# At the border between attention and MLP: other places for the norm's sum, the residual's scaling, the sums of z's quarters and the reciprocal

## The chip, the cores and the metric

The kernel runs on one core of a Trainium2 chip. The core has a matrix engine (TensorE, PE in the profile; its weight loads are listed apart as PEld), a vector engine (VectorE, DVE), an activation engine (ScalarE, ACT), a general engine (GpSimd, POOL) and an engine that here only issues transfers (SyncE, SP). Each works through its own list of instructions in order and waits on semaphores where an instruction needs another engine's result or a transfer. The metric is the device time of one execution in microseconds; the kernel before has a median of 644.58 us over three runs (643.77 to 645.73).

## The reference, cut to what matters

One decoder layer for 512 tokens of width 1024, all in float32: attention in three groups of heads, then a squared-ReLU MLP, each behind an RMS norm and each added to the residual.

```
def rms_norm(x, gain):
    y = xf * lax.rsqrt(jnp.mean(xf * xf, axis=-1, keepdims=True) + EPS)
    return (y * gain)

def mixer_sublayer(...):
    ...
    y = jnp.concatenate([y_moba, y_fox, y_dil], axis=-1) @ w_out
    return x + y

def mlp_sublayer(x, norm_g, w_up, w_down):
    hn = rms_norm(x, norm_g)
    return x + jnp.square(jax.nn.relu(hn @ w_up)) @ w_down
```

w_up is 1024 x 4096 and w_down 4096 x 1024. Since the MLP's activation is the square of a ReLU, the norm's factor 1/sqrt(v) (v is a token's mean square plus epsilon) can be left out of the products and comes out as 1/v at the end.

## The kernel before, in words

**Products in three passes.** Every float32 operand is split into a high and a low part of a type that TensorE multiplies in one pass, and a product is hi*hi + hi*lo + lo*hi. ScalarE writes a weight tile's high part (`whi`, L118), VectorE its low part (`wlo`, L119: raw minus high). Both lie in three buffers; a `Stream` object splits two pieces ahead of TensorE and loads further ahead, and a buffer is written again when TensorE has finished with the tile three before.

**Up to the border.** After attention, `x2` is the residual (eight tiles of 128 features x 512 tokens). `out_product` adds W_out's result to it in four parts; as the last two parts finish, `out_done` makes of each tile: zf (x2 times the norm's gain), its parts zh and zl, and its square. The squares of four tiles each are to be added up in two tiles `ssq`: ScalarE writes the first square into it, and the other three (`sq`, four buffers) are added by a GpSimd transfer with an adding destination (L757), so three and three transfers, each waiting for the one before it on the same tile.

**The MLP.** Its first block of 512 hidden features is an ordinary product (`up0`): 32 steps of three matmuls, four accumulators; steps 0 to 7 use weights k = 0, 1, steps 8 to 23 k = 2 to 5, steps 24 to 31 k = 6, 7, where an accumulator is finished at steps 25, 27, 29 and 31 and goes through `up_done` (copy to `c`, L853; square, L841; high part, L844; low part, L845). Then follow eight periods u = 1 to 8. In a period the up products of block u are done by a scheme of seven half-size products in place of eight (numbers 1 to 7, 24 matmuls each, L872) between four down items of block u - 1 (d00, d01, d10, d11; 24 matmuls each, L913), in the order `PERIOD = (1, 5, "d00", 2, 6, "d01", 3, 7, "d10", 4, "d11")`. The seven products need sums of z's quarters: `t_sum` (L806, VectorE) builds them for products 5, 6, 7 and 4, `t_split` (L818 ScalarE, L819 VectorE) their parts t5, t6, t7 and, for 4, a new zh and zl.

**The norm.** `x2_stats` multiplies the two `ssq` tiles with a tile of ones (L825, two float32 products in a bank of PSUM) and makes v2 (L826). `scale_x2` multiplies each tile of x2 by v2 (L831); the down results are added to that (L922), and near the end everything is multiplied by rv = 1/v2 (`RECIPROCAL`, L943).

**What sets the order.** TensorE's instructions stand in the order in which the program writes them. The instructions of the other engines are put in order by a scheduler, which keeps an instruction's needs ahead of it but can move it to and fro; `keep_in_program_order` holds one at the place where it is written. Tiles of a pool that is closed are given to pools opened later: pool `zfp` (zf, ssq, sq) is closed after step 20 of `up0`, and pool `hp` (h tiles, `c`) takes its place, so that the first write to a `c` waits for the transfers that read `sq`.

Of the kernel before, what the change touches and what calls it, by code (L numbers as in the profile page):

```python
# [11 lines left out]
F32 = mybir.dt.float32  # L12
# [6 lines left out]
P = 128  # L19
D = 1024  # L20
S = 512
# [135 lines left out]
def hymba_block(ctx: ExitStack, tc: tile.TileContext, a, out):  # L157
    nc = tc.nc
# [9 lines left out]
    def bank(tag):  # L168
        return psum.tile([P, 512], F32, name=tag, tag=tag)
# [23 lines left out]
    for c in range(len(IN_CHUNKS)):  # L193
        src = a[f"w_in{c}"]
        n = src.shape[2]
# [39 lines left out]
    for u in range(1, 9):  # L235
        for what in PERIOD:
            if isinstance(what, str):
                c, p = int(what[1]), int(what[2])
                k = 4 * (u - 1) + 2 * p
# [7 lines left out]
    def product(first, ks, operands, banks_n, done, G=2):  # L247


        n = len(ks)  # L250
        acc = [None] * banks_n
        head, tail = list(range(min(G, n))), list(range(max(G, n - G), n))
        mid = [k for k in range(n) if k not in head and k not in tail]
        order = [(k, b) for b in range(banks_n) for k in head]
        order += [(k, b) for k in mid for b in range(banks_n)]
        order += [(k, b) for b in range(banks_n) for k in tail]
        if first == 0:

            wh, wl = w.take(0)
            acc = [bank("acc") for _ in range(banks_n)]  # L260
            for m in (0, 2, 1):
                for b in range(banks_n):
                    pairs, view = operands(ks[0], b, wh, wl)
                    lhs, rhs = pairs[m]
                    nc.tensor.matmul(view(acc[b]), lhsT=lhs, rhs=rhs, start=(m == 0), stop=False)
            order = [(k, b) for k, b in order if k > 0]
        for k, b in order:
            wh, wl = w.take(first + k)
            if acc[b] is None:
                acc[b] = bank("acc")  # L270
            pairs, view = operands(ks[k], b, wh, wl)
            dst = view(acc[b])
            for m, (lhs, rhs) in enumerate(pairs):
                nc.tensor.matmul(  # L274
                    dst, lhsT=lhs, rhs=rhs, start=(k == 0 and m == 0), stop=(k == n - 1 and m == 2)
                )
            if k == n - 1:
                done(b, acc[b])
            yield
# [428 lines left out]
    for c, (kind, i) in enumerate(IN_CHUNKS):  # L708
        done = {"g": lambda i: g_done, "qk": lambda i: qk_parts[i][0], "v": v_done}[kind](i)
        n = a[f"w_in{c}"].shape[2]  # L710
# [65 lines left out]
    v2 = mlp.tile([P, S], F32, name="v2")  # L776
    rv = mlp.tile([P, S], F32, name="rv")
# [2 lines left out]
    zstack = ExitStack()  # L780
    zpool = zstack.enter_context(tc.tile_pool(name="zfp", bufs=1, side="right"))
    zf = zpool.tile([P, NK, S], F32, name="zf")
    ssq = [zpool.tile([P, S], F32, name=f"ssq{m}") for m in range(2)]
    for c, part, ks in OUT_ORDER[2:]:
        for _ in product(out_first[c, part], ks, out_operands, 4, out_done(c, part)):
            pass
# [11 lines left out]
    def t_sum(n):  # L798
        t = mlp_pools["sum"].tile([P, 4, HALF], F32, name="wsum")
        first, second = {  # L800
            5: (zf[:, lo4, t1], zf[:, lo4, t0]),
            6: (zf[:, hi4, t1], tsum.get(5)),
            4: (zf[:, hi4, t0], tsum.get(6)),
            7: (zf[:, hi4, t1], zf[:, lo4, t1]),
        }[n]
        nc.vector.tensor_tensor(t, first, second, op=ALU.subtract)  # L806
        tsum[n] = t
        if n == 4:

            hi, lo = zh[:, lo4, t1], zl[:, lo4, t1]  # L810
        else:
            hi, lo = (tp.tile([P, 4, HALF], F32R, name=f"t{n}{m}") for m in "hl")
        zop[n] = (hi, lo)
        return n

    def t_split(n):
        hi, lo = zop[n]
        nc.scalar.copy(hi, tsum[n])  # L818
        nc.vector.tensor_tensor(lo, tsum[n], hi.bitcast(F32), op=ALU.subtract)  # L819

    def x2_stats():

        ps = bank("m")
        for m in range(2):
            nc.tensor.matmul(ps, lhsT=ones, rhs=ssq[m], start=(m == 0), stop=(m == 1))  # L825
        nc.vector.tensor_scalar(v2, ps, 1.0 / D, EPS, op0=ALU.mult, op1=ALU.add)  # L826

    def scale_x2(k):


        nc.vector.tensor_tensor(x2[:, k], x2[:, k], v2, op=ALU.mult)  # L831
# [3 lines left out]
    def h_tiles(u):  # L835
        for p in range(2):
            h_at[u, p] = [hp.tile([P, 2, S], F32R, name=f"h{m}{p}", bufs=2) for m in "hl"]
# [21 lines left out]
    def up_product(u, n):  # L859

        wh, wl = w.take_made(up_first[u, n])
        bh, bl = zop[n]
        slot, first = {1: ("x", True), 6: ("x", False), 7: ("x", False), 4: ("x", False),
                       5: ("v", True), 3: ("v", False), 2: ("y", True)}[n]
        if first:
            slots[slot] = bank("m")
        acc = slots[slot]
        for f in range(2):
            for j in range(4):
                lh, ll = (x[:, j, f * P : (f + 1) * P] for x in (wh, wl))  # L870
                for m, (lhs, rhs) in enumerate(((lh, bh[:, j]), (lh, bl[:, j]), (ll, bh[:, j]))):
                    nc.tensor.matmul(  # L872
                        acc[:, f * HALF : (f + 1) * HALF], lhsT=lhs, rhs=rhs,
                        start=first and (f, j, m) == (0, 0, 0), stop=(f, j, m) == (1, 3, 2), skip_group_check=True,
                    )
        up_parts(u, n, acc)
# [24 lines left out]
    def down_item(q, c, p):  # L901
        hi, lo = h_at[q, p]
        first = down_first[q, c, p]
        if p == 0:
            down_acc[c] = [None] * 4
        for b in range(4):
            if p == 0:
                down_acc[c][b] = bank("acc")
            acc = down_acc[c][b]
            for k in range(2):  # L910
                wh, wl = (x[:, b * P : (b + 1) * P] for x in w.take(first + k))
                for m, (lhs, rhs) in enumerate(((wh, hi[:, k]), (wh, lo[:, k]), (wl, hi[:, k]))):
                    nc.tensor.matmul(acc, lhsT=lhs, rhs=rhs, start=(p, k, m) == (0, 0, 0), stop=(p, k, m) == (1, 1, 2))  # L913
            if p == 1:
                down_done(q, c, b, acc)
# [10 lines left out]
                (nc.sync, nc.scalar)[m].dma_start(rows[:, cols], dst[:, cols])  # L926

    for n, _ in enumerate(product(up0_first, list(range(NK)), up_operands, 4, up_done)):
        if n == 0:
            for m in (5, 6, 7):  # L930
                t_sum(m), t_split(m)
            t_sum(4)
        if n == 20:
            x2_stats()
            zstack.close()
            hp = ctx.enter_context(tc.tile_pool(name="hp", bufs=1, side="right"))
            h_tiles(0)
    t_split(4)
    for u in range(1, 9):
        if u < 8:  # L940
            h_tiles(u)
        if u == 5:
            nc.vector.reciprocal(rv, v2)  # L943
        for what in PERIOD:
            if isinstance(what, str):
                down_item(u - 1, int(what[1]), int(what[2]))
            elif u < 8:
                up_product(u, what)
            if u == 1 and what in (1, 5):
                for k in range(4):  # L950
                    scale_x2(k + (4 if what == 5 else 0))


def bias_tables():
# [64 lines left out]
```

## Time and profile before

| | us |
|---|---|
| median of three runs | 644.58 |
| the three runs | 644.58, 643.77, 645.73 |
| the profiled execution | 646.33 |
| its span, first to last instruction | 644.6 |
| TensorE busy in the span | 631.2 (98%) |
| VectorE busy | 460.6 (71%) |
| ScalarE busy | 322.5 (50%) |
| GpSimd busy | 43.7 (7%) |
| mean granted clock of TensorE, of full speed | 0.995 |

The trace was taken in one execution; its times count from the span's start. Busy shares are means over stages of different kinds. A line of the timeline gives an instruction's start, its duration, its engine, line, operation and tiles, and in brackets how long the engine was idle before it and what ended that. TensorE's matmuls overlap, so their pace is read from the distance of starts, not from durations. The chain of waits lists what released what, from the span's end backwards.

### The profile page before, as it was taken

Reading aid. Unit: us, or ns where it says so; the run is one execution under the profiler, and the core shown is the slowest. Engines: PE = TensorE matmul, PEld = TensorE weight load, DVE = VectorE, ACT = ScalarE, POOL = GpSimd, SP = SyncE. Lnnn points to the kernel's source line nnn. Section 1 sums busy time; section 2 is a strip of 40 time slices with the busy share of each in tenths; the row PEclk is TensorE's granted clock in tenths of the full one; section 3 lists DMA queues with packets and bytes.
Section 4 is the critical chain, followed back from the end, with each engine's and each line's share of the span. In section 5 each row is a group of like instructions: output and inputs, shape, how many; then the busy total and the mean of one; then the engine's idle time right before and its main releaser. Section 6 shows DMA issues by size and latency. Waiting matters only on the chain.

```text
span 644.6 us, 9830 instructions
## 1 busy us (share of the span) xinstructions
PE 631.2 (98%) x3800; PEld 558.4 (87%) x3800; DVE 460.6 (71%) x786; ACT 322.5 (50%) x575; POOL 43.7 (7%) x63
## 2 busy tenths in 40 slices
PE   7999999999999999999799999999999999999997
PEld 6798898898898998887599889898989899989886
DVE  6794695696588564769799766677586766865872
ACT  7457765766776676359244333333334333434320
POOL 4010210120120100001000000000000000000000
PEclk8999999999999999999899999999999999999999
DMA  8524333433421453276316143232522333212213
GB/s 315 160 91 138 115 83 75 123 91 112 118 83 50 118 160 116 67 262 130 99 33 196 40 158 99 75 99 89 164 84 60 120 99 130 66 34 67 67 39 125
DMA packets 24911, 70.03 MB, mean 109 GB/s; under 512 B 3210, under 2 KB 4762, under 8 KB 24864
## 3 DMA queue, kind: packets, MB, share of 16 engines
q1 hardware_dynamic: 18224, 57.84, 28.2%
q10 hardware_dynamic: 4432, 5.77, 3.7%
q0 software_dynamic: 2208, 5.79, 3.7%
q8 instruction: 30, 0.49, 0.3%
q14 instruction: 17, 0.14, 0.1%
HBM read 61.51 MB, written 2.11 MB: 99 GB/s over the span
## 4 chain that ended last, share of the span: by engine, by line
PE 72%; DVE 7%; ACT 3%; DMA 3%; issue 1%; POOL 0%; ACTq 0%; DVEq 0%; POOLq 0%
PE acc L913 28%; PE m L872 22%; PE acc L274 16%; DMA ssq<-sq 3%; PE m L514 2%; PE m L565 2%; PE m L541 1%; DVE ptl L548 1%; PE m L495 1%; DVE qkss L400 1%; DVE wlo L119 1%; DVE qks L418 1%; DVE m L526 1%; DVE qkraw L413 1%; ACT whi L118 1%
## 5 line engine op out<-in xcount | busy, mean ns | idle before, releaser
L118 ACT CAST whi<-wraw 128x1024 fp32r<-128x1024 f32 (+3 forms) x66 | 66.6, 1013 | 87.1 <-PE acc L913 40.5
L274 PE MATMUL acc<-whi,xh 128*128 128x512 f32 (+3 forms) x284 | 103.5, 364 | 0.7 <-DVE fl L436 0.4
L913 PE MATMUL acc<-hh,wlo 128*128 128x512 f32 x256 | 101.4, 396 | 0.0
L913 PE MATMUL acc<-hl,whi 128*128 128x512 f32 x256 | 101.3, 396 | 0.0
L913 PE MATMUL acc<-hh,whi 128*128 128x512 f32 x256 | 101.0, 395 | 0.0
L119 DVE TENSOR_TENSOR wlo<-wraw,whi 128x1024 fp32r<-128x1024 f32 (+3 forms) x66 | 78.9, 1197 | 30.2 <-ACT whi L118 29.5
L274 PE MATMUL acc<-wlo,xh 128*128 128x512 f32 (+3 forms) x284 | 95.7, 337 | 0.7 <-DVE wlo L119 0.6
L274 PE MATMUL acc<-whi,xl 128*128 128x512 f32 (+3 forms) x284 | 95.8, 337 | 0.0
L872 PE MATMUL m<-zh,whi 128*128 128x256 f32 x224 | 62.5, 279 | 0.0
L872 PE MATMUL m<-zh,wlo 128*128 128x256 f32 x224 | 62.4, 278 | 0.0
L872 PE MATMUL m<-zl,whi 128*128 128x256 f32 x224 | 62.4, 278 | 0.0
L274 PEld LDWEIGHTS acc<-whi,xl 128*128 128x128 f32 x284 | 53.6, 189 | 5.2
L913 PEld LDWEIGHTS acc<-hh,wlo 128*128 128x128 f32 x256 | 48.3, 189 | 10.8
L274 PEld LDWEIGHTS acc<-wlo,xh 128*128 128x128 f32 x284 | 54.0, 190 | 3.7 <-DVE wlo L119 1.5
L913 PEld LDWEIGHTS acc<-hl,whi 128*128 128x128 f32 x256 | 48.3, 189 | 10.1
L274 PEld LDWEIGHTS acc<-whi,xh 128*128 128x128 f32 x284 | 53.7, 189 | 3.8 <-DVE vs L430 0.7
L913 PEld LDWEIGHTS acc<-hh,whi 128*128 128x128 f32 x256 | 48.3, 189 | 9.9
L118 ACT CAST whi<-wsum 128x1024 fp32r<-128x1024 f32 x28 | 29.4, 1049 | 49.9 <-PE m L872 36.4
L119 DVE TENSOR_TENSOR wlo<-wsum,whi 128x1024 fp32r<-128x1024 f32 x28 | 34.1, 1220 | 23.0 <-ACT whi L118 23.0
L922 DVE TENSOR_TENSOR x<-acc,x 128x512 f32<-128x512 f32 (+1 forms) x65 | 42.5, 677 | 10.3 <-PE acc L913 9.6
L528 ACT ACTIVATE p<-m,mn 128x128 f32<-128x128 f32 (+1 forms) x64 | 33.6, 527 | 24.4 <-DVE mn L526 22.7
L872 PEld LDWEIGHTS m<-zh,whi 128*128 128x128 f32 x224 | 42.1, 188 | 1.2
(189 smaller groups left out, 1330.0 us busy)
## 6 DMA issues: line engine op xcount, KB each, us to landing
wraw<-in_w_down SPq DMA_DIRECT2D x32, 512.0 KB, 3.6
ublk<-in_w_up SPq DMA_DIRECT2D x28, 512.0 KB, 4.0
wraw<-in_w_in SPq DMA_DIRECT2D x21, 512.0 KB, 3.9
stk<-stk ACTq DMA_DIRECT2D x32, 128.0 KB, 2.3
wraw<-in_w_out SPq DMA_DIRECT2D x6, 512.0 KB, 4.1
alibi<-in_alibi POOLq DMA_DIRECT2D x10, 256.0 KB, 3.4
x<-in_xT SPq DMA_DIRECT2D x4, 512.0 KB, 5.8
wraw<-in_w_up SPq DMA_DIRECT2D x4, 512.0 KB, 4.9
```

What stands on the lines that cost most here:

```text
L118: nc.scalar.copy(hi, raw)
L119: nc.vector.tensor_tensor(lo, raw, hi.bitcast(F32), op=ALU.subtract)
L274: nc.tensor.matmul(dst, lhsT=lhs, rhs=rhs, start=(k == 0 and m == 0), stop=(k == n - 1 and m == 2))
L400: nc.vector.tensor_reduce(ss, sq.rearrange("p (h d) -> p h d", d=DH), axis=AX.X, op=ALU.add)
L413: nc.vector.tensor_tensor(raw, raw, state["y"][:, t].unsqueeze(2).broadcast_to([P, 8, DH]), op=ALU.mult)
L418: nc.vector.tensor_tensor(split[:, :, 1], raw, split[:, :, 0].bitcast(F32), op=ALU.subtract)
L514: nc.tensor.matmul(ps[:, :n], lhsT=st[0][:, i * P : (i + 1) * P], rhs=st[m][:, :n], start=(m == 1), stop=(m == 2 and h < FOX0),)
L528: nc.scalar.activation(p, ps[:, :n], AF.Exp, bias=mn, scale=-1.0, accum_out=st["den"][:, i : i + 1])
L565: nc.tensor.matmul(ot[:, j * P :], lhsT=v, rhs=p, start=(half == 0 and j == 0), stop=(half == 1 and j == 3))
L872: nc.tensor.matmul(acc[:, f * HALF : (f + 1) * HALF], lhsT=lhs, rhs=rhs, start=first and (f, j, m) == (0, 0, 0), stop=(f, j, m) == (1, 3, ...
L913: nc.tensor.matmul(acc, lhsT=lhs, rhs=rhs, start=(p, k, m) == (0, 0, 0), stop=(p, k, m) == (1, 1, 2))
L922: nc.vector.tensor_tensor(dst[:, cols], acc[:, cols], dst[:, cols], op=ALU.add)
```

## The change

Five edits. The two `ssq` tiles no longer have memory of their own but use v2's and rv's. The sums and splits of z's quarters for products 5, 6 and 7 are written at steps 8, 13 and 18 of `up0` instead of all at step 0, and that for product 4 at step 20. The two products with ones move from behind step 20 of `up0` to behind product 5 of period 1. The eight scalings of x2 are written behind products 2 and 6 of period 1 instead of behind 1 and 5. The reciprocal is held at the place where it is written, the start of period 5.

```diff
-    ssq = [zpool.tile([P, S], F32, name=f"ssq{m}") for m in range(2)]
+    ssq = [v2, rv]
...
     for n, _ in enumerate(product(up0_first, list(range(NK)), up_operands, 4, up_done)):
-        if n == 0:
-            for m in (5, 6, 7):
-                t_sum(m), t_split(m)
-            t_sum(4)
+        if n in (8, 13, 18):
+            m = {8: 5, 13: 6, 18: 7}[n]
+            t_sum(m), t_split(m)
         if n == 20:
-            x2_stats()
+            t_sum(4)
             zstack.close()
...
         if u == 5:
-            nc.vector.reciprocal(rv, v2)
+            tc.keep_in_program_order(nc.vector.reciprocal(rv, v2))
...
-            if u == 1 and what in (1, 5):
+            if u == 1 and what == 5:
+                x2_stats()
+            if u == 1 and what in (2, 6):
                 for k in range(4):
-                    scale_x2(k + (4 if what == 5 else 0))
+                    scale_x2(k + (4 if what == 6 else 0))
```

Three places show what the scheduler makes of it. First VectorE in the middle of `up0`: `t5l` to `t7l` belong to the quarters' sums, `wlo<-wraw` are the low parts of `up0`'s weights for k = 4, 5 and for k = 6, 7, `wlo<-ublk` those of period 1's product 1.

```order
 L749 TENSOR_TENSOR zl<-zf,zh 128x512
+L119 TENSOR_TENSOR wlo<-wraw,whi 128x1024
 L819 TENSOR_TENSOR t5l<-wsum,t5h 128x1024
 L819 TENSOR_TENSOR t6l<-wsum,t6h 128x1024
+L119 TENSOR_TENSOR wlo<-wraw,whi 128x1024
 L806 TENSOR_TENSOR wsum<-zf 128x1024
-L119 TENSOR_TENSOR wlo<-wraw,whi 128x1024 x2
+L119 TENSOR_TENSOR wlo<-ublk,whi 128x1024
 L819 TENSOR_TENSOR t7l<-wsum,t7h 128x1024
```

The first low part of a weight moves up past three instructions (t5l, t6l and the sum for product 7), the second past one. On ScalarE the high part for k = 4, 5 moves up past the high parts of t5 and t6 in the same way.

Second ScalarE at the end of `up0`, before and then now: `zh<-wsum` is product 4's high part, `whi<-wsum` the weights' high part of period 1's product 5, `c<-acc` the copies of `up0`'s results.

```order
L818 CAST zh_3456<-wsum_3662 128x4x256
L118 CAST whi_3775<-wsum_3773 128x1024
L853 COPY c_3782<-acc_3640 128x512
L853 COPY c_3793<-acc_3671 128x512
L844 CAST hh0_3751<-c_3782 128x512
```

```order
L818 CAST zh_3456<-wsum_3739 128x4x256
L853 COPY c_3776<-acc_3638 128x512
L118 CAST whi_3769<-wsum_3767 128x1024
L853 COPY c_3787<-acc_3649 128x512
L844 CAST hh0_3745<-c_3776 128x512
```

The first copy, which waits for the adding transfers, now stands ahead of product 5's weights.

Third VectorE from the last result of `up0` into period 1, before and then now: `wlo_3827` and `wlo_3821` are d00's weights, `wlo_3933` and `wlo_3923` d01's, `x2<-x2,v2` the scalings.

```order
L831 TENSOR_TENSOR x2_3016<-x2_3016,v2_3458 128x512 x3
L119 TENSOR_TENSOR wlo_3894<-ublk_3726,whi_3893 128x1024
L216 TENSOR_TENSOR wsum_3902<-wsum_3773,ublk_3638 128x1024
L943 RECIPROCAL rv_3459<-v2_3458 128x512
L119 TENSOR_TENSOR wlo_3905<-wsum_3902,whi_3904 128x1024
L119 TENSOR_TENSOR wlo_3933<-wraw_3768,whi_3932 128x1024
```

```order
L119 TENSOR_TENSOR wlo_3821<-wraw_3674,whi_3820 128x1024
L845 TENSOR_TENSOR hl1_3748<-c_3809,hh1_3747 128x512
L119 TENSOR_TENSOR wlo_3884<-ublk_3716,whi_3883 128x1024
L218 TENSOR_TENSOR wsum_3992<-ublk_3716,wsum_3892 128x1024
L826 TENSOR_SCALAR v2_3458<-m_3878 128x512
L119 TENSOR_TENSOR wlo_3895<-wsum_3892,whi_3894 128x1024
L831 TENSOR_TENSOR x2_3016<-x2_3016,v2_3458 128x512 x8
L119 TENSOR_TENSOR wlo_3923<-wraw_3762,whi_3922 128x1024
```

The eight scalings, before spread from the middle of `up0` on, now stand in one row directly ahead of d01's weights, and the reciprocal has left this place; it stands in period 5, directly ahead of that period's d00 weights. From period 2 on the engines' lists are otherwise as they were.

## Rows read from the trace of the kernel before

**Rows 1.** Chain of waits around the border: start us, us, engine, tiles, line.

```profile
293.81 5.99 DMA ssq<-sq
300.87 4.30 DMA ssq<-sq
305.70 4.04 DMA ssq<-sq
310.27 3.29 DMA ssq<-sq
313.60 1.13 PE m L825 x2
```

**Rows 2.** Waits of TensorE: who waited for whom, us in total, times, longest.

```profile
PE m L825 <- DMA ssq<-sq: 2.8, 1, 2.8
...
PE acc L274 <- DVE wlo L119: 1.9, 2, 1.2
```

**Rows 3.** Timeline of TensorE through `up0`: start us, us, what [idle before].

```profile
294.50 0.39 PE L274 MATMUL acc<-zh,whi 128*128 128x512 f32 x1
...
305.04 0.39 PE L274 MATMUL acc<-zl,whi 128*128 128x512 f32 x1
306.63 0.51 PE L274 MATMUL acc<-zh,wlo 128*128 128x512 f32 x1 [1.20 <-DVE wlo L119]
...
309.74 1.02 PE L825 MATMUL m<-ssq,ones 128*128 128x512 f32 x2
313.60 1.13 PE L825 MATMUL m<-ssq,ones 128*128 128x512 f32 x2 [2.85 <-DMA ssq<-sq]
...
323.72 0.28 PE L872 MATMUL m<-zh,whi 128*128 128x256 f32 x1
```

**Rows 4.** Stretches: us, busy of each engine, then TensorE's granted clock, DMA, GB/s.

```profile
306.00:309.00 3.00, 2.37 (x10) 1.98 (x11) 3.00 (x4) 0.78 (x1) 0.56 (x1) 1.00 0.68 82
...
314.00:318.00 4.00, 4.00 (x11) 2.87 (x10) 2.42 (x3) 0.00 (x0) 0.00 (x0) 0.59 0.00 0
```

**Rows 5.** The same view, periods 1 and 2.

```profile
323.70:366.10 42.40, 42.40 (x267) 38.19 (x266) 39.00 (x47) 17.44 (x23) 0.00 (x0) 1.00 0.33 100
366.10:408.30 42.20, 42.20 (x267) 38.01 (x266) 29.75 (x35) 16.01 (x20) 0.00 (x0) 1.00 0.32 100
```

**Rows 6.** Timeline of VectorE, the same columns as rows 3.

```profile
301.00 0.69 DVE L749 TENSOR_TENSOR zl<-zf,zh 128x512 fp32r<-128x512 f32 x1 [0.70 <-ACT zh L748]
...
304.23 1.22 DVE L806 TENSOR_TENSOR wsum<-zf 128x1024 f32<-128x1024 f32 x1
305.36 2.35 DVE L119 TENSOR_TENSOR wlo<-wraw,whi 128x1024 fp32r<-128x1024 f32 x2
...
329.12 1.90 DVE L831 TENSOR_TENSOR x<-x,v 128x512 f32<-128x512 f32 x3
...
333.20 3.35 DVE L943 RECIPROCAL rv<-v 128x512 f32<-128x512 f32 x1
...
494.04 1.22 DVE L119 TENSOR_TENSOR wlo<-wraw,whi 128x1024 fp32r<-128x1024 f32 x1
```

**Rows 7.** Timeline of ScalarE.

```profile
300.87 1.04 ACT L818 CAST t5h<-wsum 128x1024 fp32r<-128x1024 f32 x1
...
302.77 2.00 ACT L118 CAST whi<-wraw 128x1024 fp32r<-128x1024 f32 x2
...
319.80 0.59 ACT L853 COPY c<-acc 128x512 f32<-128x512 f32 x1 [0.66 <-PE acc L274]
```

**Rows 8.** Timeline of SyncE's queue: loads that the low parts released.

```profile
306.61 0.33 SPq L95 DMA_DIRECT2D wraw<-in_w_down  x1
307.74 0.33 SPq L95 DMA_DIRECT2D wraw<-in_w_down  x1
```

**Rows 9.** Timeline of TensorE at d00 of period 5.

```profile
498.52 0.40 PE L913 MATMUL acc<-hh,wlo 128*128 128x512 f32 x1
```

More of the change, by code (lines that the diff above doesn't have):

```diff
@@ L928, in hymba_block @@
     for n, _ in enumerate(product(up0_first, list(range(NK)), up_operands, 4, up_done)):
-        if n == 0:
-            for m in (5, 6, 7):
-                t_sum(m), t_split(m)
+        if n in (8, 13, 18):
+            m = {8: 5, 13: 6, 18: 7}[n]
+            t_sum(m), t_split(m)
+        if n == 20:
             t_sum(4)
-        if n == 20:
-            x2_stats()
             zstack.close()
```

## The prediction

> **What bounds the kernel now.** I read the chain of waits first. It ends in TensorE from the border on: from 313.60 us nothing but matmuls stands in it, and ahead of that four adding transfers ssq<-sq and the second product with ones [rows 1]. So every microsecond that TensorE stands still or runs slowly at the border is a microsecond of the whole, and nothing else there is. The stretches of the MLP say the same: in periods 1 and 2 TensorE is busy for the full 42.40 and 42.20 us, with VectorE at 39.00 and 29.75 [rows 5]; what is gained at the border can't be given back to another engine there as long as the weights' low parts come in time.
>
> The waits of TensorE name two causes at the border: 2.8 us of the product with ones for a transfer, and, of 1.9 us in two pieces, one wait of 1.2 us for a weight's low part (wlo) [rows 2, 3]. The timeline gives their place. The pace of a matmul is read between 294.50, the first of step 1, and 305.04, the second of step 16, 46 matmuls later: 10.54 / 46 = 0.2291 us. Step 16 is the first on weights k = 4, 5, whose low part VectorE begins only at 305.36, behind the quarter sum of 304.23 [rows 6].
>
> The stretches give the third cause. From 306 to 309, behind the 1.2 us gap, the granted clock is 1.00; from 314 to 318, behind the gap of 2.85 us, it is 0.59, that is mostly the lower of the two levels, 1.2 in place of 2.4 GHz [rows 4].
>
> **What the border costs now.** At step 16: from 305.04 to 309.74 lie 14 matmul distances, 14 x 0.2291 = 3.21, and it took 4.70: 1.49 us lost. From the first product with ones at 309.74 to period 1's first matmul at 323.72 it took 13.98. In it are 11 steps, 33 x 0.2291 = 7.56, and the two products with ones: a product shows as two records, 1.02 us for both, of which by the lone matmuls' tail some 0.16 overlaps what follows, so 0.86 each and 1.72 for two. 13.98 - 7.56 - 1.72 = 4.70 lost: 2.85 idle and 1.85 by the lower clock. Together 1.49 + 4.70 = 6.19 us.
>
> **The change part by part.**
>
> *The quarters' sums.* VectorE's low part for k = 4, 5 moves up past three instructions. Its high part on ScalarE can start where t5's did, at 300.87, ends after 1.05 at 301.92, and the low part follows the zl of 301.00 at 301.95 and ends at 303.2; TensorE wants it for step 16's third matmul at 305.27. Spare: 2 us, so 1.49 us go. The next two weights: by 1.13 us from start to start of such an instruction ((2.35 - 1.22) in the pair at 305.36 [rows 6]) the list gives 306.6 for k = 6, 7 (wanted at 310.8) and 308.8 for product 1 (wanted at 315.8).
>
> *The products with ones.* They keep their 1.72 us, but at period 1 behind product 5. The last transfer landed at about 313.6 [rows 1]. Without the gaps `up0` ends at 294.50 + 93 x 0.2291 = 315.8, products 1 and 5 (2.85 us each: a pair takes 5.7 in the chain) at 321.5, and only then are the sums wanted: 8 us of cover. The gap of 2.85 and the low clock's 1.85 behind it go. d00 starts at 323.2.
>
> *What is late next.* The wait does not vanish; it moves to ScalarE. The first copy c<-acc takes over memory that the transfers read (pool hp behind pool zfp), so it waits for the last of them. Before, it ran at 319.80 and was held by TensorE, not by that [rows 7]. Now step 25 ends near 311.9, the transfer at 313.6, so ScalarE stands for 1.7 us, with product 5's high part queued behind the copy. I replay both lists from there with the trace's distances: 1.13 us for a wide and 0.60 for a narrow VectorE instruction ((1.90 - 0.69) / 2, the three at 329.12 [rows 6]), 0.95 for a wide cast (2.00 - 1.05 [rows 7]), 0.5 for a narrow one. Copy 313.65 to 314.24, high part until 315.2, low part until 316.4; product 5 wants it at 318.9: spare 2.5. VectorE then runs without a pause: eight instructions to d00's low part, which ends at 322.3 and is wanted at 323.7, d00's third matmul: spare 1.4. That is the tightest place, and up to a landing of 313.6 + 1.4 = 315.0 the moved wait costs nothing.
>
> *The scalings.* Eight in a row, 8 x 0.60 = 4.8 us, stand ahead of d01's low part. They start at about 326.8, the low part ends at 332.8, d01 wants it at 335.0: spare 2.1, cost nothing. Behind them the additions of d01's results (L922) find x2 scaled in time.
>
> *SyncE's queue.* The load that follows k = 4, 5 went out at 306.61 and goes now at about 303.2, the next at 306.6 in place of 307.74 [rows 8]; both are only wanted in periods 1 and 2. They now lie beside the fourth and fifth transfer. Before, two loads lay beside the fifth, and it took 4.04; the second took 5.99 [rows 1]. The bounds of one transfer are so 3.29 and 5.99; I take what each took before.
>
> *The reciprocal.* Its 3.35 us [rows 6] leave VectorE's row in period 1, where they cost nothing, and stand in period 5 directly ahead of d00's low part, which before started at 494.04 for a matmul of 498.52 [rows 6, 9]. Starting 3.3 later it ends at 498.5, and the weights must still be loaded: 0.2 us late. Between 0 (list a little earlier) and 0.6 (semaphores, 0.1 for each of four); I take 0.2.
>
> *Sharing memory* (ssq in v2 and rv) adds no instruction; rv is overwritten only in period 5, v2 behind the products.
>
> **The sum.** -1.49 - 2.85 - 1.85 + 0.2 = -6.0 us. The profiled execution took 646.33 for a span of 644.6, so 1.73 lie around the span; with the change 640.3 and a span of 638.6. It stands 1.75 above the median of 644.58, which I take as a difference of executions; on the median the sum gives 638.6 us, 0.93% less.
>
> **The rivals.**
>
> *Late sums, smaller gain.* If the fourth and fifth transfer, now beside the loads sent earlier, each took the 5.99 of the second, the last would land at 313.6 + 1.69 + 1.95 = 317.2, 2.2 us past the spare. TensorE would wait 2.2 us at d00 and the gain be 3.8: 640.8 us. For it: that 5.99 had a load beside it. Against: the fifth had two and took 4.04. The Trainium skill (its first page, Trainium Kernel Development and Optimization, section Key Constraints) says that transfers issued from SP, ACT and POOL all run on the same 16 engines and interleave; by that rule this rival would be the likeliest, and the sum 640.8. The trace bears it out in the second transfer and not in the fifth.
>
> *Slower: the wait comes back doubled.* If all three last transfers took 5.99, the last would land at 319.9. Product 5's low part would end at 322.8, 3.9 us after it is wanted, and d00's 1.1 us later still: 5.0 idle, the first piece longer than the 2.85 behind which the clock fell. With one fall of 1.85 that is 6.9, with two 8.7, against 6.0 gained: 645.5 to 647.3, at the likeliest 646.6. It decides from a landing at about 319 on. Against: a third transfer of 5.99 with only the tail of a load beside it; the last took 3.29.
>
> *No change: the next list is full.* VectorE runs without a pause from 314 to 333 in my replay. A further wait in that row, say for a load (the sum for period 2's product 5 stands in it ahead of d10's low part), of over 3.5 us past its spare, and TensorE stands with it: 642.7 to 646.5. Against: in period 1 before, VectorE was at 39.00 of 42.40 without one wait of TensorE [rows 5].
>
> **How the numbers follow.** Forecast 0.74, late sums 0.15, no change 0.06, slower 0.05. The forecast's own range: the spare and the transfers' phase move the gain by 1 us, the median by some 1 (the runs spread from 643.77 to 645.73): 637.2 to 640. The range goes on to the late sums with their share of spread and leaves out no change and slower: 637.0 to 642.0. About 0.3%, 1.9 us, is what a measurement of this kernel tells from no change. The forecast and the late sums are faster by more than that, 0.88 with some of the latter's tail taken off; within it 0.07; slower 0.05.
>
> **What would show it.** Right: no wait of TensorE on L825 and none on wlo at step 16; the clock at 1.00 from 294 on; period 1's first matmul at 315.8, period 2's at 359.9 in place of 366.10; the first copy c released by the last transfer at 313 to 315; the span about 638.6. Wrong: that landing past 315 with TensorE's idle time at d00 or product 5 of period 1; a clock below 1.00 near 320; over 0.5 us of waiting for wlo in period 5.

## The result and the profile after

The changed kernel took 640.29 us in the median of 5 runs (639.80 to 640.73). The kernel before, on the same chip, took 645.73 us (643.77 to 647.94). The measured ratio is 0.9906, with a 95% interval of 0.9884 to 0.9927, or 0.94% less; the quotient of these two medians alone is 0.9916, or 0.84% less. Forecast were 0.93% and 638.6 us. The profiled execution has a span of 638.0 us; 638.6 was forecast for it.

The page of the changed kernel shows the span and, in the row PEclk, the granted clock in 40 equal slices:

```profile
span 638.0 us, 9834 instructions
...
PEclk9999999999999999999999999999999999999999
```

Every slice of the clock reads 9. The chain of waits of the changed kernel (start us, us, engine, tiles, line) is matmuls alone across the border:

```profile
275.21 40.61 PE acc L274 x177
315.82 5.70 PE m L872 x48
...
359.59 5.60 PE m L872 x48
```

Where [rows 1] had four adding transfers and a product with ones, one piece of 40.61 us runs from the attention's last projections into period 1. Of TensorE's own waits (who waited for whom, us in total, times, longest) the largest is:

```profile
PE acc L274 <- DVE wlo L119: 2.2, 2, 1.6
```

The wait of L825 for a transfer, 2.8 us in [rows 2], is gone. The 2.2 us for wlo lie at the kernel's start in both of their pieces, at 11.65 and 20.75 us; none is at step 16. The timeline of TensorE (start us, us, what) answers to [rows 3]:

```profile
293.44 0.40 PE L274 MATMUL acc<-zh,whi 128*128 128x512 f32 x1
...
315.66 0.28 PE L872 MATMUL m<-zh,whi 128*128 128x256 f32 x1
...
321.36 1.02 PE L825 MATMUL m<-v,ones 128*128 128x512 f32 x2
322.22 1.02 PE L825 MATMUL m<-rv,ones 128*128 128x512 f32 x2
...
323.53 0.40 PE L913 MATMUL acc<-hh,wlo 128*128 128x512 f32 x1
```

From step 0 of `up0` to period 1's first matmul it takes 315.66 - 293.44 = 22.22 us. In the kernel before it took 323.72 - 293.59 = 30.13. Of the 7.91 us between them, 1.72 are the two products with ones, which now stand behind product 5; 6.19 us are saved. That is to the hundredth the 1.49 + 4.70 that the prediction counted as lost there. The rest of the 6.6 us between the spans is 0.15 us at the border's start and 0.26 us behind it: from period 1's first matmul on, 644.6 - 323.72 = 320.88 us before, and 638.0 - 315.66 - 1.72 = 320.62 after. The agreement to the hundredth says that nothing of the losses counted in that one execution is left. How large they are in other executions is another matter, as the first experiment shows.

The stretches (us, busy of each engine, then the granted clock, DMA share, GB/s) answer to [rows 4, 5]:

```profile
306.00:309.00 3.00, 3.00 (x14) 2.45 (x14) 3.00 (x3) 1.05 (x1) 0.00 (x0) 1.00 0.94 200
314.00:318.00 4.00, 4.00 (x28) 3.67 (x28) 3.21 (x5) 3.94 (x7) 0.00 (x0) 1.00 0.02 4
315.80:358.20 42.40, 42.40 (x264) 37.56 (x263) 38.70 (x50) 19.15 (x26) 0.00 (x0) 1.00 0.32 100
```

From 314 to 318 the clock is 1.00, the higher level, where it was 0.59. Period 1 (third line) keeps TensorE full, although VectorE has 50 instructions in it in place of 47.

### The profile page after: what moved, and what is told of

Same layout as the page of the kernel before. It is cut to its first block, busy times and chain, and to the rows that moved or that the text cites. A ratio compares the mean times of both kernels' runs of the same rounds, so it can differ in the third digit from the quotient of the medians.

```text
span 638.0 us, 9834 instructions
## 1 busy us (share of the span) xinstructions
PE 627.6 (98%) x3800; PEld 556.3 (87%) x3800; DVE 460.2 (72%) x786; ACT 322.4 (51%) x575; POOL 43.9 (7%) x63
## 4 chain that ended last, share of the span: by engine, by line
PE 77%; DVE 7%; ACT 1%; issue 1%; ACTq 0%; POOL 0%; DVEq 0%
PE acc L913 28%; PE m L872 22%; PE acc L274 20%; PE m L514 2%; PE m L565 2%; PE m L541 1%; DVE ptl L548 1%; PE m L495 1%; DVE qkss L400 1%; DVE wlo L119 1%; DVE qks L418 1%; DVE m L526 1%; DVE qkraw L413 1%; DVE qkv L401 1%; DVE osum L582 0%
```

## The experiments

All are timed against the kernel before in the same series of runs. That kernel's median was 646.4 to 646.5 us there, so ratios are compared, and spans with spans. A ratio given here can differ by up to 0.0007 from the quotient of the two medians. The first four share one series, the next four another; the last stands by itself.

### The quarter sums at step 0 again

```diff
-        if n in (8, 13, 18):
-            m = {8: 5, 13: 6, 18: 7}[n]
-            t_sum(m), t_split(m)
-        if n == 20:
+        if n == 0:
+            for m in (5, 6, 7):
+                t_sum(m), t_split(m)
             t_sum(4)
+        if n == 20:
             zstack.close()
```

> The changed kernel with one edit undone: all four sums of z's quarters are written at step 0 of up0 again; the product with ones stays in period 1. Theory (my prediction's sum): VectorE's low part for k = 4, 5 again stands behind t5l, t6l and a quarter sum, TensorE waits about 1.2 us at step 16, no clock falls, and nothing else is late: period 1 begins 1.5 us later than in the changed kernel (at about 317.1 against 315.66), span about 639.5, 0.23% over the changed kernel, 0.7% under the kernel before. Rival (the sums' places are worth nothing, the scheduler sorts them by need): span 638.0 and no wait for wlo at step 16.

Measured: 641.35 us (641.26 to 642.28), ratio 0.9922 [0.9908, 0.9937], span 639.5. The timeline of TensorE has the wait at step 16, but a short one:

```profile
294.40 0.40 PE L274 MATMUL acc<-zh,whi 128*128 128x512 f32 x1
...
306.54 0.50 PE L274 MATMUL acc<-zh,wlo 128*128 128x512 f32 x1 [0.30 <-DVE wlo L119]
...
317.19 0.28 PE L872 MATMUL m<-zh,whi 128*128 128x256 f32 x1
```

The border, from step 0 to period 1, took 22.79 us: 0.57 more than in the changed kernel, not 1.49. The timelines of ScalarE point to the reason. First the kernel before:

```profile
299.82 0.63 ACT L756 ACTIVATE sq<-x 128x512 f32<-128x512 f32 x1 [0.79 <-DMA ssq<-sq]
...
300.87 1.04 ACT L818 CAST t5h<-wsum 128x1024 fp32r<-128x1024 f32 x1
```

Then this experiment:

```profile
299.75 0.61 ACT L756 ACTIVATE sq<-x 128x512 f32<-128x512 f32 x1
...
300.78 1.04 ACT L818 CAST t5h<-wsum 128x1024 fp32r<-128x1024 f32 x1
```

In the kernel before ScalarE stood 0.79 us for the second transfer, the one that took 5.99 us [rows 1], ahead of the last squares; everything behind was that much later. Here the second transfer was out of the way in time, and TensorE's border began 0.81 us later (294.40 in place of 293.59), while t5's high part came at the same time. So the early quarter sums cost the border 0.57 us in this execution, and 1.49 where the second transfer was slow. The slow one was no single case: in the third experiment, which has the border of the kernel before, ScalarE stood 0.77 us there and step 16 lost 1.48. Which of the two is usual is not shown. Between the medians of the spans the edit is worth 1.05 us (639.55 in four runs, 638.5 in the changed kernel's five). The span came out where it was expected, but the rest of its 1.5 us lay ahead of the border (0.96 us, some 0.7 of it a wait of the attention for a transfer), where this edit does nothing. The scheduler also put product 5's high part ahead of the first copy again (312.49 and 314.46); TensorE waits there in neither kernel.

### The product with ones behind step 20

```diff
+            x2_stats()
             zstack.close()
...
-            if u == 1 and what == 5:
-                x2_stats()
```

> The changed kernel with the product with ones back behind step 20 of up0; the quarter sums stay spread. Theory (a wait swallows what is gained ahead of it): TensorE reaches the product 1.5 us earlier than in the kernel before, the last adding transfer still lands at about 313.6 to 314, so TensorE idles 4.3 to 4.8 us there in place of 2.85 and then runs some 4 us at the lower clock (1.85 us lost): span 644 to 645, as before, ratio 0.998 to 1.001. Rival (the two gains add up): the spread sums alone bring 1.5 us, span 643.1, ratio 0.9977, with an idle time of 2.85 us as before.

Measured: 646.74 us (642.30 to 649.26, 12 runs), ratio 0.9998 [0.9978, 1.0019], span 645.1. TensorE, then the stretches 310 to 314 and 314 to 318:

```profile
314.02 2.07 PE L825 MATMUL m<-rv,ones 128*128 128x512 f32 x2 [5.01 <-DMA rv<-sq]
```

```profile
310.00:314.00 4.00, 0.00 (x0) 0.00 (x0) 1.22 (x1) 1.04 (x1) 0.86 (x1) 0.65 0.45 91
314.00:318.00 4.00, 3.98 (x7) 2.49 (x8) 1.87 (x3) 0.00 (x0) 0.00 (x0) 0.50 0.00 0
```

All other edits of the change are in this kernel, and together they gain nothing. What the sums give at step 16 is waited away a little later, since the transfer lands when it lands: 5.01 us in place of 2.85, where 4.3 to 4.8 were expected. The 2.16 us between them are the 1.49 won at step 16, a border that began 0.28 earlier and a transfer that landed 0.42 later, which makes 2.19. Behind it the clock falls to 0.50, the lower level. The product's place behind the last landing is the change's main part. A theory that adds up the edits one by one falls here.

### The wait filled with matmuls

The kernel before, with twelve matmuls that nobody reads between the two products with ones:

```diff
+FILL = 12
...
+            if m == 0:
+                spare = bank("m")
+                for _ in range(FILL):
+                    nc.tensor.matmul(spare, lhsT=zh[:, 0, :P], rhs=zh[:, 0], start=True, stop=True)
```

> The kernel before, with 12 matmuls that nobody reads (128 x 512, one pass) between the two products with ones, so that TensorE works through most of the wait for the transfer: 12 x 0.229 = 2.75 us. Theory (the lower clock follows from the standstill): the idle time falls from 2.85 to about 0.1 us, the granted clock stays at 1.00 from 314 to 318, and the 1.85 us of the lower clock are saved although the matmuls themselves bring nothing: span 642.8, ratio 0.9972. Rival (the clock falls for another reason, such as the float32 product or the change of stage): the clock is below 0.7 from 314 to 318 again, span 644.6 to 644.8, ratio 1.000.

Measured: 645.01 us (644.47 to 645.56, 10 runs), ratio 0.9982 [0.997, 0.9993], span 642.7. TensorE, and the stretch from 314 to 318:

```profile
310.04 3.33 PE L830 MATMUL m<-zh 128*128 128x512 f32 x12
313.46 1.12 PE L826 MATMUL m<-ssq,ones 128*128 128x512 f32 x2
...
321.99 0.28 PE L877 MATMUL m<-zh,whi 128*128 128x256 f32 x1
```

```profile
314.00:318.00 4.00, 4.00 (x18) 3.13 (x17) 3.37 (x5) 1.50 (x2) 0.00 (x0) 1.00 0.02 4
```

The second product starts when it did in the kernel before, 313.46 against 313.60 [rows 3]: the transfer is waited for as long. But TensorE is not idle meanwhile, the clock stays at 1.00 where it was 0.59, and the border, from 293.44 on, takes 321.99 - 293.44 = 28.55 us, 1.58 less than before. So the low clock came from the standstill and was a cost of its own, as the prediction had counted it: 1.85 us there, 1.58 here. The other 3.12 of its 4.70 us belong to the wait, where it had 2.85.

### The reciprocal left free

```diff
-            tc.keep_in_program_order(nc.vector.reciprocal(rv, v2))
+            nc.vector.reciprocal(rv, v2)
```

> The changed kernel without holding the reciprocal: the scheduler puts its 3.35 us into period 1, ahead of the low part of product 7's weights and of d10's. Theory (the row of VectorE has room for it there): the two low parts end at 341 and 345 against 342.5 and 346 wanted, no wait of TensorE; the 0.1 us that it costs in period 5 goes: span 637.9 to 638.0, the same as the changed kernel. Rival (holding it back is what keeps the row in time): TensorE waits 1 to 3 us for a low part in period 1, span 639 to 641 and perhaps a lower clock behind it.

Measured: 640.13 us (639.83 to 641.23), ratio 0.9903 [0.9888, 0.9918], span 638.0. On VectorE it runs in period 1:

```profile
336.86 3.34 DVE L942 RECIPROCAL rv<-v 128x512 f32<-128x512 f32 x1
```

TensorE waits for nothing there. Holding the reciprocal back is worth nothing, with the sums spread as they are.

### A seventh transfer

The changed kernel with its last adding transfer made twice; the last tile's squares so count twice in the norm.

```diff
                     nc.gpsimd.dma_start(total, sq, accum_op=ALU.add)
+                    if k == 7:
+                        nc.gpsimd.dma_start(total, sq, accum_op=ALU.add)
```

> The changed kernel with the last adding transfer made twice (the last tile's squares are counted twice): the chain of transfers ends some 3.9 us later, at about 317.8 in place of 313.9. Theory (the wait has moved to the first copy of up0's results, with about 0.9 us of spare to TensorE): the first copy starts at 317.9, product 5's low part ends at 320.6 against 318.7 wanted and d00's 1.1 us later still, so TensorE waits some 3.0 us in two pieces for wlo in period 1, and none for the product with ones; span 641.0, and 642.9 if the clock falls behind the first piece; ratio 0.995 to 0.998. Rival (the sums are wanted only by the product with ones, at 321.4, so that 7.5 us of lateness are free): span 638.0, ratio 0.9905.

Measured: 644.01 us (643.87 to 646.47, 5 runs), ratio 0.9961 [0.9947, 0.9974]. Four spans are 642.1 to 642.4, between the 641.0 without and the 642.9 with a fall of the clock that were expected; the profiled one, 644.7, is the longest. It shows TensorE's waits, ScalarE's first copy, and the stretches 318 to 324 and 324 to 330:

```profile
321.26 0.38 PE L874 MATMUL m<-t5h,whi 128*128 128x256 f32 x1 [1.67 <-ACT whi L118]
322.52 0.58 PE L874 MATMUL m<-t5h,wlo 128*128 128x256 f32 x1 [0.76 <-DVE wlo L119]
```

```profile
319.68 0.58 ACT L855 COPY c<-acc 128x512 f32<-128x512 f32 x1 [6.53 <-PE m L874]
320.16 1.05 ACT L118 CAST whi<-wsum 128x1024 fp32r<-128x1024 f32 x1
```

```profile
318.00:324.00 6.00, 3.57 (x23) 3.16 (x22) 3.45 (x5) 4.26 (x7) 0.00 (x0) 0.82 0.06 10
324.00:330.00 6.00, 6.00 (x23) 4.63 (x23) 6.00 (x8) 4.89 (x8) 0.00 (x0) 0.61 0.09 14
```

The copy is put down to a matmul, but those of L874 had run since 316.60; what it stood for, 6.53 us, was the seventh transfer, issued at 315.49 and 4.0 us long. Product 5's high part is queued behind the copy, its low part behind that, and TensorE waits for both, at product 5 of period 1 and not at L825. So the wait that the change took from TensorE did move to ScalarE's first copy, and comes back to TensorE when the last landing is late. Behind 1.67 and 0.76 us of standstill the clock fell to 0.61: the slower rival's mechanism, here made by a late landing. It does not go on to d00 as the prediction and the expectation had it: in the slow clock TensorE came to d00 too late to wait there.

### One product with ones, the tiles added on GpSimd

```diff
-        for m in range(2):
-            nc.tensor.matmul(ps, lhsT=ones, rhs=ssq[m], start=(m == 0), stop=(m == 1))
+        nc.gpsimd.tensor_tensor(v2, v2, rv, op=ALU.add)
+        nc.tensor.matmul(ps, lhsT=ones, rhs=v2, start=True, stop=True)
```

> The changed kernel with the two tiles of sums added by GpSimd (one 128 x 512 addition) and one product with ones in place of two. Theory (TensorE is the bound, so 0.86 us of its work less is 0.86 us less in all; GpSimd has 6 us from the last transfer's landing to the product): span 637.1 to 637.2, ratio to the kernel before 0.0013 below that of the changed kernel (0.9903 to 0.9906), so 0.989. Rival (GpSimd's addition beside VectorE's full row around 315 us slows that row past its spare of 0.9 us at d00): TensorE waits for a low part in period 1 and the span stays at 638 or more.

Measured: 640.04 us (639.74 to 640.38), ratio 0.9899 [0.9884, 0.9915], span 638.3. GpSimd's addition, VectorE beside it, and the matmul of d00 that waits:

```profile
314.65 1.29 POOL L824 TENSOR_TENSOR v<-v,rv 128x512 f32<-128x512 f32 x1 [2.57 <-DMA rv<-sq]
```

```profile
315.23 1.26 DVE L841 SCALAR_TENSOR_TENSOR c<-c 128x512 f32<-128x512 f32 x1 [1.69 <-ACT c L853]
```

```profile
323.57 0.50 PE L913 MATMUL acc<-hh,wlo 128*128 128x512 f32 x1 [0.61 <-DVE wlo L119]
```

The product saves 0.86 us of TensorE's row and 0.61 come back as a wait. The low part of d00's weights begins at 322.30, 0.93 us later than in the changed kernel. VectorE's instruction beside the addition takes 1.26 us where the changed kernel's takes 0.69, but that is the smaller part: about 0.25 us by the rows, since product 5's high part was ready at 316.14 and its low part began at 316.42. The rest came from the last transfer, which landed later (the first copy starts at 314.61, not at 313.92). And without the second product TensorE wants the low part 0.74 us earlier (at 322.79, one distance of 0.23 behind the matmul of 322.56, not at 323.53), so that of 0.94 us of spare only 0.20 was left. The rival's outcome came, a wait for a low part and a span over 638, but its cause only in part: without any slowing of VectorE the low part would by these rows still have been an estimated 0.5 us late.

### GpSimd additions in place of the adding transfers

The kernel before, with the six transfers replaced:

```diff
-                    nc.gpsimd.dma_start(total, sq, accum_op=ALU.add)
+                    nc.gpsimd.tensor_tensor(total, total, sq, op=ALU.add)
```

> The kernel before, with the six adding transfers replaced by six additions on GpSimd (128 x 512 each), the product with ones at its old place. Theory (it is the lateness of the transfers that costs, not the place of the product): the sums are ready by about 303 us, TensorE has no wait for L825 and no fall of the clock (4.7 us), ScalarE doesn't wait for a square's buffer either (0.8 us off the wait at step 16): span 639.0 to 639.5, ratio 0.991 to 0.992, and the runs lie within 1 us of each other in place of 3.5. Rival (GpSimd's additions and VectorE hinder each other): VectorE's wide instructions between 288 and 303 us take over 1.22 us, the wait for wlo at step 16 grows by 1 to 4 us: span 640.5 to 643.

Measured: 646.06 us (644.99 to 647.97, 12 runs), ratio 0.9998 [0.9985, 1.001], span 644.0. That is beyond both expectations. GpSimd, VectorE and TensorE:

```profile
290.20 1.33 POOL L757 TENSOR_TENSOR ssq<-ssq,sq 128x512 f32<-128x512 f32 x1 [0.37 <-ACT sq L756]
291.86 1.38 POOL L757 TENSOR_TENSOR ssq<-ssq,sq 128x512 f32<-128x512 f32 x1 [0.32 <-ACT sq L756]
```

```profile
290.61 1.48 DVE L749 TENSOR_TENSOR zl<-zf,zh 128x512 fp32r<-128x512 f32 x1 [0.23 <-ACT zh L748]
292.01 2.32 DVE L806 TENSOR_TENSOR wsum<-zf 128x1024 f32<-128x1024 f32 x1
294.25 0.68 DVE L749 TENSOR_TENSOR zl<-zf,zh 128x512 fp32r<-128x512 f32 x1
```

```profile
295.63 0.47 PE L274 MATMUL acc<-zh,whi 128*128 128x512 f32 x1 [1.20 <-issue]
...
310.75 0.51 PE L274 MATMUL acc<-zh,wlo 128*128 128x512 f32 x1 [2.37 <-DVE wlo L119]
...
313.86 1.88 PE L825 MATMUL m<-ssq,ones 128*128 128x512 f32 x4
...
323.14 0.28 PE L872 MATMUL m<-zh,whi 128*128 128x256 f32 x1
```

No wait is left at the products with ones, and the clock is 1.00. From the first of them to period 1 it takes 323.14 - 313.86 = 9.28 us in place of 13.98: the 4.70 us that the prediction counted come back whole, by another way than the product's place. But VectorE is held up beside each addition, and TensorE loses 4.12 us ahead of the products: 0.68 before `up0`, where its matmuls of W_out already ran that much later, 1.36 at `up0`'s first matmul (295.63; the trace names no engine for that wait), 0.80 in steps 0 to 15 and 1.28 at step 16, where the wait for wlo grows to 2.37 us. The cause of one wait is removed and another engine's list pays for it. The trace names VectorE's low parts for the wait at step 16 and for one of 0.38 us at step 0; that its list is also behind the 1.36 us is argued from its late rows, not shown.

The same additions and the single product in the changed kernel:

> The changed kernel with all seven additions on GpSimd in place of transfers, and one product with ones. Theory: the first copy waits for TensorE alone (starts at about 312), VectorE's row gets 1.9 us more spare, and TensorE has 0.86 us less to do: span 637.1, ratio 0.989, like the kernel with one product and transfers, since the spare was enough there. Rival (as for the additions on GpSimd in the kernel before): VectorE is slowed around 290 to 303 us, and TensorE waits for wlo at step 16: span 638 to 640.

Measured: 642.59 us (642.36 to 644.02), ratio 0.9944 [0.993, 0.9957]: slower than the changed kernel, and beyond both expectations. The profiled execution is the longest of the five (span 642.2; the others have 640.6 to 641.3). TensorE, and the stretch from 298 to 300:

```profile
296.44 0.47 PE L274 MATMUL acc<-zh,whi 128*128 128x512 f32 x1 [1.22 <-issue]
...
297.52 0.50 PE L274 MATMUL acc<-zh,wlo 128*128 128x512 f32 x1 [0.38 <-DVE wlo L119]
```

```profile
298.00:300.00 2.00, 2.00 (x7) 1.54 (x6) 2.00 (x5) 2.00 (x5) 0.57 (x1) 0.51 0.69 193
```

VectorE is slowed as in the kernel before with these additions, but the expected wait at step 16 is not there. TensorE stands at step 0, and behind that the clock falls to 0.51: the nine matmuls from 297.86 take 3.65 us, where the changed kernel's take 2.07. The four shorter executions have no profile, so what they lose stays open.

### One product with ones, the tiles added on VectorE

```diff
-        for m in range(2):
-            nc.tensor.matmul(ps, lhsT=ones, rhs=ssq[m], start=(m == 0), stop=(m == 1))
+        tc.keep_in_program_order(nc.vector.tensor_tensor(v2, v2, rv, op=ALU.add))
+        nc.tensor.matmul(ps, lhsT=ones, rhs=v2, start=True, stop=True)
...
-            if u == 1 and what == 5:
+            if u == 1 and what == "d00":
                 x2_stats()
...
```

The scalings of x2 stand behind product 6 and behind d01 here.

> The changed kernel, but VectorE adds the two tiles of sums into one (behind the low part of d01's weights) and one product with ones follows in place of two, one place later, behind d00; the scalings of x2 stand behind product 6 and behind d01. Theory (TensorE bounds from the border on, and VectorE's list has room behind d00): one product, 0.86 us, leaves TensorE's row and one addition of about 0.6 us enters VectorE's, without the lengthening that the addition on GpSimd caused; no wait of TensorE for d00's or d01's low part over 0.2 us; span about 637.1, ratio about 0.989 against the kernel before, 0.5 to 0.9 us below the changed kernel. Rival (the list is full): the scalings now lie among the additions of d01's results and h's work for period 2, and TensorE waits for hl or a low part between 325 and 360 us for as long as was saved; span 637.8 to 639, ratio 0.9905 to 0.992.

Measured: 640.76 us (639.21 to 641.93, 6 runs), ratio 0.9908 [0.989, 0.9925], profiled span 637.4. In the profile the theory holds: no new wait of TensorE stands in it, VectorE's addition takes 0.69 us, and from period 1's first matmul (315.76) to the end it takes 321.64 us in place of 322.34. But the last transfer landed early in it: the first copy, at 311.88, waited for TensorE and not for the transfer, so this profile doesn't show the list under a landing as late as the changed kernel's. The six spans run from 637.4 to 640.2 (median 639.0), the five of the changed kernel from 638.0 to 639.0 (median 638.5). The time shows no gain; where the longer runs lose it stays open, since the profile is one of the short ones.

## Why the prediction was right, step by step

**The idle time and the low clock at the products with ones** (2.85 and 1.85 us) were read rightly, and as one cause with two costs: filling the wait without shortening it gave back 1.58 us, and putting the product back brought all of it, and more. The additions on GpSimd, which leave the product where it was and have the sums ready earlier, gave back the same 4.70 us there. What decides is the product's place behind the last landing; the division between the two costs was 3.12 and 1.58 rather than 2.85 and 1.85. The other edits could show no gain without it. No run undoes the sharing of memory or the scalings' place by itself.

**The wait at step 16** was taken for a property of the code, which it is only in part. The 1.49 us were read from one execution, in which the second transfer took 5.99 us and held ScalarE by 0.79. With that transfer in time the early sums cost 0.57 us. The sum came out because it was compared with that same execution, and the change removes the wait whatever its length.

**The transfers.** The working took for each the time it had before. Only the last repeated. GpSimd's queue of the changed kernel shows when they were issued:

```profile
288.15 0.94 POOL L757 DMA_DIRECT2D v<-sq  x1 [22.55 <-DMA wraw<-in_w_up]
292.95 0.89 POOL L757 DMA_DIRECT2D v<-sq  x1 [3.86 <-DMA v<-sq]
297.37 0.86 POOL L757 DMA_DIRECT2D v<-sq  x1 [3.53 <-ACT zf L747]
297.91 1.21 POOL L757 DMA_DIRECT2D rv<-sq  x1
304.89 0.86 POOL L757 DMA_DIRECT2D rv<-sq  x1 [5.77 <-DMA rv<-sq]
310.53 0.86 POOL L757 DMA_DIRECT2D rv<-sq  x1 [4.78 <-DMA rv<-sq]
```

From issue to landing the six took 4.2, 3.9, 5.7, 6.4, 5.1 and 3.3 us. The longest lies outside the bounds of 3.29 and 5.99 that the working gave for one transfer. The fourth and fifth, beside the earlier loads, were long, as the rival of the late sums had it; but the second took 3.9 in place of 5.99, and the last, with 3.3 us as before, landed at 313.9 where 313.6 was worked out. Behind the short second transfer the fourth was issued 2.96 us earlier (297.91, before 300.87 [rows 1]); the fourth and fifth then took 3.2 us longer together. That these made up for each other is luck. The forecast and that rival were nearer to each other than the chances of 0.74 and 0.15 say.

**What is late next** was named rightly: the first copy. ScalarE and VectorE of the changed kernel, with two rows that answer to [rows 6, 7]:

```profile
313.92 0.59 ACT L853 COPY c<-acc 128x512 f32<-128x512 f32 x1 [2.50 <-DMA rv<-sq]
```

```profile
300.91 1.23 DVE L119 TENSOR_TENSOR wlo<-wraw,whi 128x1024 fp32r<-128x1024 f32 x1 [0.16 <-ACT whi L118]
...
315.48 1.22 DVE L119 TENSOR_TENSOR wlo<-wsum,whi 128x1024 fp32r<-128x1024 f32 x1 [0.26 <-ACT whi L118]
...
321.37 1.22 DVE L119 TENSOR_TENSOR wlo<-wraw,whi 128x1024 fp32r<-128x1024 f32 x1
```

Step 16's low part runs at 300.91 (301.95 was forecast). Product 5's ends at 316.70 (316.4), d00's at 322.59 (322.3), and d00's third matmul wants it at 323.53. The spare is 0.94 us, not 1.4. The seventh transfer took more than that, and TensorE waited. The eight scalings take 4.90 us (4.8) from 327.11 on, and TensorE waits for nothing behind them.

**The reciprocal** costs d00 of period 5 a distance of 0.33 us between two matmuls, 491.98 to 492.31, in place of the usual 0.23: 0.1, where 0.2 was taken and 0 to 0.6 allowed; no run shows the 0.1 us for each semaphore in that upper bound. That holding it back gains something the prediction did not claim, and it doesn't.

**The median.** The working took 638.6 from the median of 644.58. On the chip of the result the kernel before had 645.73, so the same 6.0 us would give 639.7; 5.44 were measured between the medians. The measured 640.29 lies above the 637.2 to 640 that the prediction gave as the forecast's own range, and nearer to the 640.8 of the late sums, but the trace shows none of that rival's waits. What was off is mostly the median of three runs from which the sum was taken, 1.15 us below that of five; that 0.93% and 0.94% agree is in part luck. The kernel before spreads over 3.5 us (644.16 to 647.63 in 22 runs of the first series), the changed one over 0.9 in its five. One profile of a kernel whose waits hang on a transfer is one draw out of that spread.

## What to carry to other kernels

Where one wait for a transfer ends a stage, nothing gained ahead of it counts, so move what waits first, and only then tune what lies before it. Count the standstill and the slow clock behind it as two costs, and look for where the wait goes: here to a copy that takes over the transfer's memory, with 0.94 us to spare. A wait read from one profile can hold both what the order costs and what a slow transfer added; undo the edit alone, and look at more than one execution, to tell them apart. And when work is taken off the bounding engine, subtract it from the spare of whatever is wanted behind it: with one product with ones, 0.20 of 0.94 us were left.

## What the runs showed of the hardware

A GpSimd addition with two inputs and VectorE's instructions with two inputs ran one after the other, not side by side. In the experiment with GpSimd additions VectorE's zl was issued at 290.61, while the addition ran until 290.20 + 1.33 = 291.53, and it ended at 292.09, 0.56 us later; alone it takes 0.68. The wide sum of 292.01 ended 1.09 us behind the next addition's end; alone it takes 1.22. The Trainium skill (page SBUF — State Buffer, section SBUF: two separate sides) calls the two engines' shared port pair an exclusive lock, held for the whole instruction; these rows agree. The adding transfers, in [rows 6] and in the changed kernel, lengthen no such instruction.

Adding transfers of 256 KB each took between 3.3 and 6.4 us within one execution, that of the changed kernel.

The clock did not follow the pauses alone. Pauses of 1.20 and 0.38 us in the first three matmuls of `up0`, in the kernel before with GpSimd additions, left it at 1.00 (296 to 306); 1.22 and 0.38 at the same matmuls of the changed kernel with them were followed by 0.51 from 298 to 300 and 0.63 from 300 to 302. A single pause of 2.37 us left it at 1.00 (310 to 318), one of 2.85 was followed by 0.59 [rows 4], one of 5.01 by 0.50, and 1.67 and 0.76 close together, with the seventh transfer, by 0.61 from 324 to 330. What tells the first two cases apart no run here settles.
